# Gate stage of a two-layer encoder: staged weights fetched one set ahead, the low halves of the gate weights on VectorE, the cast of the merged activations one chunk later

## The chip, the cores and the metric

The kernel runs on one NeuronCore of a Trainium2 chip. The metric is the device time of one execution in microseconds (us); the median of three runs is given. Engines: PE (TensorE, matmuls), DVE (VectorE), ACT (ScalarE), POOL (GpSimd) and SP (SyncE, which here only issues transfers). Each engine takes its instructions in the order of the program and waits on semaphores for the others.

## The reference, cut to what matters

Two consecutive layers over 1,056 tokens (1,024 of a prompt, 32 of a running stream), 1,024 channels, float32. The part around the change is the merge behind attention (branch a) and spatial gating (branch b):

```
q, k, v, qi, ki, wi, u, vg, ga, gb = split(x @ w_in)
merged = sigmoid(ga) * (o_a @ w_pa) + sigmoid(gb) * (o_b @ w_pb)
x = LN1(ALPHA * x + merged @ w_out)
x = LN2(ALPHA * x + square(relu(x @ w_ff1)) @ w_ff2)
```

## The kernel before, in words

**Numbers.** Every matrix operand is cut into a high half (the value cast to fp32r) and a low half (value minus high half). A product takes three matmuls: high x high, high x low, low x high (`mac3`, L563 to L565).

**Tiles.** Activations lie channel by token, tokens in three chunks of 384, 384 and 288 columns. `gemm` takes one group of 128 output columns of the weights at a time (a group m), and in it chunk by chunk: all matmuls of a chunk into one PSUM bank of pool `mm` (two banks), then `evac`, which empties the bank, then some steps of a side job (`stage.step`).

**Stages of a layer.** The front (input projections, top-k selection, attention) is laid out by a planner, `Sched`. It takes task costs and priorities from the tables `CFG` (entry 0 for layer 0, entry 1 for layer 1) and writes each engine's order. Behind it stands the gate stage, written by hand in `gate_phase`: a rest of gb (one group), PB (`o_b @ w_pb`, 8 groups of 4 x 128 rows, emptied by DVE at L1792), PA (`o_a @ w_pa`, 8 groups of 4 x 128 rows, emptied by ACT at L1798) and GA (ga, 8 groups of 8 x 128 rows). Then `mixer_tail` runs five groups of `w_out` by `gemm` (emptied by DVE at L1822 and L1823) and hands the rest to the planner: last groups, norm and the MLP.

**GA's emptying.** For each chunk ACT writes the sigmoid of the bank to a work tile (L1807), DVE multiplies by PA's result and adds the gb term (L1808, L1809), and ACT casts the sum to the high half of `merged` (L1810). After the third chunk of a group DVE makes the three low halves (L1815).

**Weights.** `Stream` (`ws`) brings the weights of all these groups. `get` cuts the group after the present one and fetches the one after that: a transfer on SP's queue into one of two raw tiles (L482), then on POOL a copy for the high half (L460) and a subtraction for the low half (L468) into one of four `slab` tiles.

**The staged sums.** `Stage` is the side job: for the MLP's second matrix it loads 24 sets of four 128-row blocks by 256 columns (two transfers, L1736), makes four sums on DVE (L1746, L1747, L1749, L1750), casts the high halves on ACT (L1755), makes the low halves on DVE (L1759) and stores both to `wD` in device memory (four transfers, L1760, L1761). A set takes five steps; PB and PA run one step a chunk, GA and w_out two. Its tiles come from the pool `st` of seven buffers, handed out in turn: two raw, two high and two low per set. The transfer of the next set is issued in step 4 of the present one, behind its stores on SP.

Of the kernel before, what the change touches and what calls it, by code (L numbers as in the profile page):

```python
# [54 lines left out]
class T:  # L55
    pass


CFG = [{'PRI': {'iw': -0.263,
          'ck': -1.41,  # L60
          'ix': 0.646,
          'ie': 7.629,
          'sc': -1.88,
          'sb': 0.12,
          'sa': -3.806,
          'w0': -12.158,
          'w1': -20.884,
          'q0': 0.818,
          'q1': -0.506,
          'qe': -2.132,  # L70
          'qf': -10.943,
          'vw': -2.371,
          'vg': 0.964,
          'kw': -0.64,
          'kv': 17.749,
          'ke': -2.247,
          've': 6.527,
          'kf': -0.064,
          'sg': -6.589,
          'sh': -2.689,  # L80
          'sv': -3.979,
          'uw': 3.518,
          'u': 1.569,
          'gw': 22.568,
          'g': 8.705,
          'tk': 13.75,
          'ta': 1.653,
          'tb': 0.012,
          'td': 0.218,
          'tu': 1.174,  # L90
          'tm': 0.821,
          'tv': 0.272719516,
          'ca': -16.039,
          'cb': -3.477,
          'at': -0.61,
          'un': 0.057,
          'qk': -4.73,
          'lm': -6.346,
          'ex': -1.74,
          're': -5.398,  # L100
          'no': 6.46,
          'tr': 4.284,
          'pc': -13.59,
          'ps': 1.194,
          'pv': 6.416,
          'fi': 1.481,
          'fo': -7.008,
          'fg': 39.227,
          'fh': 9.693,
          'fw': 1.109,  # L110
          'fe': -3.641,
          'if': -3.311,
          'lt': -3.992,
          'lc': -5.237,
          'nb': 4.366,
          'nz': -7.65,
          'lv': 2.538,
          'rd': -15.758},
  'ORDER': [2, 4, 0, 3, 8, 1, 6, 5, 7],
  'IORD': [0, 5, 1, 4, 2, 3, 8, 6, 7],  # L120
  'QORD': [4, 8, 7, 3, 5, 2, 0, 6, 1],
  'KORD': [8, 3, 2, 1, 5, 7, 0, 4, 6],
  'CR': [0, 1, 2],
  'PEN': {'V': 0.82161371, 'S': 0.30937078, 'G': 0.0},
  'XPR': [4.187073758, -18.133365959, -0.385257991],
  'GLATE': 10,
  'BXK': 'mm|lg',
  'P13': 'pt',
  'P12': 'buf',
  'P11': 'buf',  # L130
  'TPK': 'tp|mm',
  'FLK': 'tp|mm',
  'BKK': 'tp|tp',
  'SGK': 'tp|lg',
  'MMK': 'mm|tp|lg',
  'MTK': 'tp|lg',
  'PVK': 'mm|tp|lg'},
 {'PRI': {'iw': 1.116,
          'ck': -1.329,
          'ix': 0.495,  # L140
          'ie': 3.337,
          'sc': -3.797,
          'sb': 0.152,
          'sa': -3.277,
          'w0': -12.127,
          'w1': 2.962,
          'q0': 1.662,
          'q1': -8.268,
          'qe': 1.253,
          'qf': -17.089,  # L150
          'vw': 6.706,
# [24 lines left out]
          'qk': -10.595,
          'lm': 22.428,
          'ex': 4.959,
          're': -5.159,
          'no': 1.164,  # L180
          'tr': -3.253,
          'pc': 1.243,
          'ps': -3.243,
          'pv': 10.918,
          'fi': 4.409,
          'fo': -0.689,
          'fg': 5.578,
          'fh': 4.434,
          'fw': 6.004,
          'fe': -4.622,  # L190
          'if': 0.401,
          'lt': 11.598,
          'lc': 20.451,
          'nb': -16.84,
          'nz': -16.864,
          'lv': -6.918,
          'rd': 5.965},
  'ORDER': [5, 4, 2, 0, 8, 1, 3, 7, 6],
  'IORD': [3, 1, 0, 4, 2, 8, 5, 6, 7],
  'QORD': [6, 5, 7, 0, 3, 1, 8, 2, 4],  # L200
  'KORD': [1, 5, 7, 0, 2, 4, 8, 3, 6],
  'CR': [0, 1, 2],
  'PEN': {'V': 0.810300138, 'S': 0.563224975, 'G': 0.448262313},
  'XPR': [-2.402896891, -8.136167056, -1.136631082],
  'GLATE': -1,
  'BXK': 'tp|lg',
  'P13': 'pt',
# [142 lines left out]
def tile_trunk(ctx: ExitStack, tc: tile.TileContext, I, O):  # L350
# [118 lines left out]

    class Stream:  # L470
        def __init__(self):
            self.items, self.used, self.dmas, self.splits, self.raws, self.out = [], 0, 0, 0, {}, {}
# [13 lines left out]
        def cut(self, i):  # L486
            while self.splits <= i:
                j = self.splits
                self.fetch(j)
                _, kt, ncol, _, place = self.items[j]  # L490
                n, raw = kt * ncol, self.raws.pop(j)
                if place is not None:
                    hi, lo = [xrow(8 * place + 4 * i, 4)[:, :, 2 * CH:2 * CH + 256] for i in range(2)]
                    split(hi, lo, raw.rearrange("p (a c) -> p a c", a=4), "g", "g")
                    self.out[j] = [[x[:, k // 2, k % 2 * 128:(k % 2 + 1) * 128] for k in range(KT)] for x in (hi, lo)]
                    self.splits += 1
                    continue
# [5 lines left out]
                split(hi, lo, raw, "g", "g")  # L503
                self.out[j] = [[x[:, k * ncol:(k + 1) * ncol] for k in range(kt)] for x in (hi, lo)]
                self.splits += 1

        def get(self, ahead=1):
            i = self.used
            self.used += 1
            self.cut(i)  # L510
            for j in range(i + 1, min(i + 1 + ahead, len(self.items))):
                if self.items[j][3]:
# [66 lines left out]
    def rhs_x(k, t0, n):  # L579
        return xh(k, t0, n), xl(k, t0, n)  # L580
# [1142 lines left out]
    class Stage:  # L1723
# [14 lines left out]
            self.fetched += 1  # L1738

        def steps(self):  # L1740
            for n, (c, mp) in enumerate(self.todo):
                if n == 0:
                    self.fetch()
                t = self.raw.pop((c, mp))
                q = [t[0][:, :, 0:128], t[1][:, :, 0:128], t[0][:, :, 128:256], t[1][:, :, 128:256]]
                V.tensor_tensor(q[3], q[2], q[3], op=OP.add)  # L1746
# [6 lines left out]
                h = [half_t("st", F32R)[:, 0:512].rearrange("p (k c) -> p k c", k=2) for _ in range(2)]  # L1753
# [12 lines left out]
        def step(self, n):  # L1766
# [2 lines left out]

    def gate_phase(L):  # L1770
        st = L.st = Stage(L.l)
        obh = hb_t(F32R)
        obl = [row_t(i, F32R) for i in LAYOUT_LO]
        for i in range(4):
# [25 lines left out]
        L.mh = a_t(F32R)  # L1800
        L.mhi = [L.mh[:, m, :] for m in range(KT)]
        L.mlo = []
        held = []

        def ev(m, t0, n, ps):
            w = work([128, CH])[:, :n]
            S.activation(w, ps, AF.Sigmoid)  # L1807
            V.tensor_tensor(w, w, p2[m][:, t0:t0 + n], op=OP.mult)  # L1808
            V.tensor_tensor(w, w, g2[m][:, t0:t0 + n], op=OP.add)  # L1809
            S.copy(L.mhi[m][:, t0:t0 + n], w)  # L1810
            held.append((t0, n, w))
            if len(held) == 3:
                L.mlo.append(row_t(LAYOUT_HI[m], F32R))
                for t0, n, w in held:
                    V.tensor_tensor(L.mlo[m][:, t0:t0 + n], w, L.mhi[m][:, t0:t0 + n].bitcast(F32), op=OP.subtract)  # L1815
                held.clear()
        gemm(KT, KT, rhs_x, ev, st)

    def residual(R):
        def ev(m, t0, n, ps):  # L1820
# [174 lines left out]
    def mixer_tail(L):  # L1995
# [524 lines left out]
```

## Time and profile before

| | us |
|---|---|
| median of three runs | 3130.18 (3125.76 to 3131.55) |
| the profiled execution | 3129.05 |
| its span, first to last instruction | 3127.3 |
| PE busy in it | 2944.9 (94%) |
| DVE busy | 2148.6 (69%) |
| ACT busy | 1370.9 (44%) |
| POOL busy | 829.0 (27%) |

The profile is of one execution. Its time is the span and about 2 us around it. A busy PE is not PE at its peak: matmuls are pipelined, and their durations overlap. So a stage is best judged by how long it takes for its number of matmuls. PEclk is the share of its full clock that PE was granted. A row of a window holds: from and to, its length, busy time (and number of instructions) of PE, PEld (PE's weight loads), DVE, ACT and POOL, PEclk, the busy share of the DMA engines and GB/s.

### The profile page before, as it was taken

The page shows a single profiled execution, that of the slowest core. Times are in us where ns is not written, and L with a number is a line of the kernel's source. Part 1 is how long each engine was busy: PE and PEld are TensorE (multiplying, and loading weights), DVE is VectorE, ACT ScalarE, POOL GpSimd, SP SyncE. Part 2 cuts the span into 40 slices and gives each one's busy share as a digit, 9 for nine tenths or more (in the row PEclk, how much of TensorE's full clock was granted, in tenths as well). Part 3 has the DMA queues.
Part 4 walks back from the last instruction along what each step waited for, and adds up shares of the span by engine and source line. Part 5 has one row for each costly group of instructions (what it writes and reads, how often), then busy time and mean ns, then how long its engine had stood idle before and what let it go on. Part 6 is the DMA issues. An engine that isn't in the chain of part 4 may idle for free.

```text
span 3127.3 us, 54780 instructions
## 1 busy us (share of the span) xinstructions
PE 2944.9 (94%) x20868; PEld 2874.2 (92%) x20868; DVE 2148.6 (69%) x4416; ACT 1370.9 (44%) x2702; POOL 829.0 (27%) x1191
## 2 busy tenths in 40 slices
PE   8999898988999999999999999989889999999998
PEld 7998898987899999999989999879788999999998
DVE  6888874465676648885479887844656766488845
ACT  5687663221343325442347865722213433254422
POOL 5733532322200001111376324433223000011023
PEclk9999999999999999999989999999899999999999
DMA  3101104545353328564111111045453533285642
GB/s 113 46 28 36 46 21 139 185 155 168 100 176 110 102 92 290 183 207 137 32 40 48 45 29 42 12 152 182 145 175 104 165 110 110 94 290 191 200 127 83
DMA packets 336023, 368.77 MB, mean 118 GB/s; under 512 B 32656, under 2 KB 257936, under 8 KB 335760
## 3 DMA queue, kind: packets, MB, share of 16 engines
q1 hardware_dynamic: 335760, 365.27, 36.6%
q8 instruction: 164, 2.69, 0.4%
q14 instruction: 99, 0.81, 0.1%
HBM read 259.05 MB, written 106.15 MB: 117 GB/s over the span
## 4 chain that ended last, share of the span: by engine, by line
PE 60%; DVE 13%; DMA 9%; ACT 3%; issue 3%; SPq 2%; POOL 2%; POOLq 0%; DVEq 0%; ACTq 0%
PE lg L1905 17%; PE tp L1905 8%; DMA st<-in_w_ff_dram 5%; PE mm L563 5%; PE mm L565 5%; PE mm L564 5%; PE mm L1905 4%; PE lg L563 2%; PE lg L565 2%; PE lg L564 2%; DVE st L1759 1%; ACT junk_a L943 1%; PE lg L1063 1%; PE lg L1064 1%; DVE J L908 1%
## 5 line engine op out<-in xcount | busy, mean ns | idle before, releaser
L943 ACT ACTIVATE junk_a<-R,sel 128x640 int8<-128x640 f32 (+6 forms) x258 | 226.3, 877 | 61.3 <-DVE sel L956 54.7
L460 POOL TENSOR_SCALAR sl<-rw 128x1024 fp32r<-128x1024 f32 (+1 forms) x92 | 90.2, 981 | 605.0 <-PE mm L564 227.1
L564 PE MATMUL mm<-R,sl 128*128 128x384 f32 (+1 forms) x722 | 236.9, 328 | 13.9 <-DVE R L1815 11.7
L563 PE MATMUL mm<-A,sl 128*128 128x384 f32 (+1 forms) x512 | 168.3, 329 | 12.6 <-DVE HB L1822 9.8
L651 POOL TENSOR_TENSOR HB<-w,HB 128x528 fp32r<-128x528 f32 x2 | 2.6, 1321 | 637.8 <-ACT HB L464 637.8
L1746 DVE TENSOR_TENSOR st<-st,st 128x256 f32<-128x256 f32 x48 | 27.1, 564 | 206.9 <-DMA st<-in_w_ff_dram 206.9
L908 DVE TENSOR_SCALAR_CACHE_REDUCE J<-R,sel 128x896 uint8<-128x896 f32 (+6 forms) x190 | 167.2, 890 | 2.4
L565 PE MATMUL mm<-A,sl 128*128 128x384 f32 (+1 forms) x512 | 166.1, 324 | 0.4 <-POOL sl L468 0.4
L468 POOL TENSOR_TENSOR sl<-rw,sl 128x1024 fp32r<-128x1024 f32 (+1 forms) x77 | 153.6, 1994 | 17.4 <-PE tp L1103 4.5
L1755 ACT CAST st<-st 128x512 fp32r<-128x512 f32 x96 | 56.8, 618 | 224.9 <-DVE st L1749 194.6
L563 PE MATMUL mm<-XB,sl 128*128 128x384 f32 (+1 forms) x456 | 153.5, 337 | 0.0
L564 PEld LDWEIGHTS mm<-R,sl 128*128 128x128 f32 x722 | 139.2, 193 | 15.1 <-DVE R L1815 12.3
L564 PE MATMUL mm<-XB,sl 128*128 128x384 f32 (+1 forms) x456 | 152.2, 334 | 0.0
L565 PE MATMUL mm<-XB,sl 128*128 128x384 f32 (+1 forms) x444 | 148.5, 335 | 0.0
L2344 DVE TENSOR_TENSOR A<-lg,A 128x528 f32<-128x528 f32 x168 | 118.4, 705 | 40.3 <-PE lg L1905 38.1
L1905 PE MATMUL lg<-R,sl 128*128 128x264 f32 x1024 | 144.1, 287 | 1.8 <-DVE A L2342 1.6
L1905 PEld LDWEIGHTS lg<-R,sl 128*128 128x128 f32 x1024 | 134.0, 191 | 2.6 <-DVE A L2342 2.0
L1091 POOL TENSOR_SCALAR sl<-sl,sm 128x640 f32<-128x640 f32 (+8 forms) x90 | 71.0, 796 | 169.1 <-DVE sm L1087 139.0
L563 PEld LDWEIGHTS mm<-A,sl 128*128 128x128 f32 x512 | 97.4, 190 | 16.3 <-DVE HB L1822 8.3
L563 PE MATMUL mm<-HB,sl 128*128 128x384 f32 (+1 forms) x262 | 88.6, 338 | 19.3 <-DVE R L1792 14.6
L2152 ACT COPY st<-lg 128x528 f32<-128x528 f32 x72 | 43.2, 600 | 142.1 <-PE lg L1905 112.5
L1905 PE MATMUL lg<-R,A 128*128 128x264 f32 x816 | 104.9, 284 | 0.0
(818 smaller groups left out, 10162.6 us busy)
## 6 DMA issues: line engine op xcount, KB each, us to landing
rw<-in_w_ff_dram SPq DMA_DIRECT2D x104, 512.0 KB, 4.7
wD<-st SPq DMA_DIRECT2D x192, 256.0 KB, 2.5
rw<-in_w_in_dram SPq DMA_DIRECT2D x60, 512.0 KB, 4.4
R<-wD SPq DMA_DIRECT2D x50, 512.0 KB, 4.5
hD<-st SPq DMA_DIRECT2D x94, 264.0 KB, 2.1
st<-in_w_ff_dram SPq DMA_DIRECT2D x96, 256.0 KB, 4.0
sl<-wD SPq DMA_DIRECT2D x46, 512.0 KB, 3.9
st<-hD SPq DMA_DIRECT2D x72, 264.0 KB, 5.6
```

Source lines behind the costliest of these rows:

```text
L460: G.tensor_scalar(o, i, 1.0, 1.0, op0=OP.mult, op1=OP.mult)
L468: {"g": G, "v": V}[e_lo].tensor_tensor(lo, src, hi.bitcast(F32), op=OP.subtract)
L563: PE.matmul(ps, ah, bh, start=first, stop=False)
L564: PE.matmul(ps, ah, bl, start=False, stop=False)
L565: PE.matmul(ps, al, bh, start=False, stop=last)
L908: V.tensor_scalar(junk[j % 2].bitcast(U8)[:p, :n], L.sc(b), thr, None, op0=op, op1=OP.add, accum_out=g.cnt[:p, j:j + 1])
L943: S.activation(junk_a[:p, :n], L.sc(b), AF.Sign, bias=g.cf[:p, j:j + 1], scale=-1.0, accum_out=g.cnt[:p, j:j + 1])
L1091: ENG[eng].tensor_scalar(self.lt[e], self.lt[e], self.ms[:, 2, e:e + 1], 1.0, op0=OP.mult, op1=OP.mult)
L1755: S.copy(h[j], t[j])
L1905: PE.matmul(bank[name, s], a[:, k, :], b, start=fresh and k == 0 and i == 0, stop=k == kt - 1 and i == 2, skip_group_check=not fresh)
L2152: S.copy(both(bx[key]), bank["B"])
L2344: V.tensor_tensor(r, b, r, op=OP.add)
```

## The change

Five edits:

- `Stage`: the first set's load is issued as before, and each set now begins with its two high tiles and the load of the set after it. The low halves overwrite the raw tiles, so a set takes four `st` buffers. The stores stand one step later than the low halves.
- `Stream`: while `late` is set (the gate stage and the five groups of w_out), POOL only copies; the subtraction goes to DVE by `follow`, which `gemm` calls after each chunk and `get` at its start. This moves 30 subtractions per layer (16 of 512 columns, 14 of 1,024).
- GA: ACT's cast of a chunk (`his_out`) stands behind the next chunk's sigmoid, and DVE's three low halves of a group (`lows_out`) behind the first add of the next group.
- `mixer_tail` clears `late` after the staged sums are done.
- The priority tables `CFG[0]` and `CFG[1]` have other numbers. In layer 0's front this changes the mixing of gb projections with attention; in layer 1 hardly any row of PE moves.

```diff
-  'BXK': 'mm|lg',
+  'BXK': 'tp|mm',
...
+                if self.late:
+                    copy("g", hi, raw)
+                    self.low.append((lo, raw, hi))
+                else:
+                    split(hi, lo, raw, "g", "g")
...
+        def follow(self):
+            for lo, raw, hi in self.low:
+                V.tensor_tensor(lo, raw, hi.bitcast(F32), op=OP.subtract)
+            self.low.clear()
...
                 if stage:
                     stage.step(kt // 4)
+                ws.follow()
...
         def steps(self):
-            for n, (c, mp) in enumerate(self.todo):
-                if n == 0:
-                    self.fetch()
+            self.fetch()
+            for c, mp in self.todo:
+                h = [half_t("st", F32R)[:, 0:512].rearrange("p (k c) -> p k c", k=2) for _ in range(2)]
+                self.fetch()
...
                 for j in range(2):
-                    lo = half_t("st", F32R)[:, 0:512].rearrange("p (k c) -> p k c", k=2)
-                    V.tensor_tensor(lo, t[j], h[j].bitcast(F32), op=OP.subtract)
+                    V.tensor_tensor(t[j], t[j], h[j].bitcast(F32), op=OP.subtract)
+                yield
+                for j in range(2):
                     nc.sync.dma_start(w[:, 0, 2 * j:2 * j + 2], h[j].bitcast(F32))
-                    nc.sync.dma_start(w[:, 1, 2 * j:2 * j + 2], lo.bitcast(F32))
-                self.fetch()
-                yield
+                    nc.sync.dma_start(w[:, 1, 2 * j:2 * j + 2], t[j])
...
+        def his_out():
+            for m, t0, n, w in his:
+                S.copy(L.mhi[m][:, t0:t0 + n], w)
+            his.clear()
...
         def ev(m, t0, n, ps):
             w = work([128, CH])[:, :n]
             S.activation(w, ps, AF.Sigmoid)
             V.tensor_tensor(w, w, p2[m][:, t0:t0 + n], op=OP.mult)
             V.tensor_tensor(w, w, g2[m][:, t0:t0 + n], op=OP.add)
-            S.copy(L.mhi[m][:, t0:t0 + n], w)
-            held.append((t0, n, w))
...
+            his_out()
+            if t0 == 0:
+                lows_out()
+            his.append((m, t0, n, w))
+            held.append((m, t0, n, w))
         gemm(KT, KT, rhs_x, ev, st)
+        his_out()
+        lows_out()
```

SP's queue in layer 0's PB, before: stores of one staged set (`wD`), then the load of the next (`st`), then weights (`rw`).

```order
L1736 DMA st_6313<-in_w_ff_dram 128x2x256
L1736 DMA st_6314<-in_w_ff_dram 128x2x256
L482 DMA rw_6350<-in_w_pb_dram 128x4x128
L1760 DMA wD_6382<-st_6383 128x512
L1761 DMA wD_6382<-st_6401 128x512
L1760 DMA wD_6382<-st_6384 128x512
L1761 DMA wD_6382<-st_6405 128x512
L1736 DMA st_6409<-in_w_ff_dram 128x2x256
L1736 DMA st_6410<-in_w_ff_dram 128x2x256
```

The same place now (L1747 is the load, L1772 and L1773 the stores).

```order
L1747 DMA st_6250<-in_w_ff_dram 128x2x256
L1747 DMA st_6251<-in_w_ff_dram 128x2x256
L482 DMA rw_6292<-in_w_pb_dram 128x4x128
L1772 DMA wD_6287<-st_6248 128x512
L1773 DMA wD_6287<-st_6244 128x512
L1772 DMA wD_6287<-st_6249 128x512
L1773 DMA wD_6287<-st_6245 128x512
L1747 DMA st_6345<-in_w_ff_dram 128x2x256
L1747 DMA st_6346<-in_w_ff_dram 128x2x256
```

The pattern on the queue is the same, but the stores of a set (here st_6244 to st_6249) now stand behind the load of the set after it (st_6250, st_6251), and are followed by the load of the one after that.

DVE in the same stage, before (L1792 empties a bank; the rest are staged sums).

```order
L1759 TENSOR_TENSOR st_6305<-st_6245,st_6282 128x512
L1759 TENSOR_TENSOR st_6309<-st_6246,st_6283 128x512
L1792 TENSOR_TENSOR R_894_5910<-mm_6317,R_894_5910 128x384
L1792 TENSOR_TENSOR R_894_5910<-mm_6331,R_894_5910 128x288
L1746 TENSOR_TENSOR st_6314<-st_6313,st_6314 128x2x128
L1747 TENSOR_TENSOR st_6313<-st_6313 128x2x128
L1792 TENSOR_TENSOR R_923_6123<-mm_6352,R_923_6123 128x384
```

And now (L1803 empties a bank, L513 is the low half of a group of weights, L1769 the low halves of a staged set).

```order
L1769 TENSOR_TENSOR st_6244<-st_6244,st_6248 128x512
L1769 TENSOR_TENSOR st_6245<-st_6245,st_6249 128x512
L513 TENSOR_TENSOR sl_6290<-rw_6228,sl_6290 128x512
L1803 TENSOR_TENSOR R_895_5902<-mm_6311,R_895_5902 128x384
L1803 TENSOR_TENSOR R_895_5902<-mm_6329,R_895_5902 128x288
L1758 TENSOR_TENSOR st_6251<-st_6250,st_6251 128x2x128
L1759 TENSOR_TENSOR st_6250<-st_6250 128x2x128
L1803 TENSOR_TENSOR R_923_6123<-mm_6355,R_923_6123 128x384
```

One subtraction per group has come into DVE's order, behind the group's first emptying.

ACT in layer 0's GA, before (L1807 sigmoid, L1810 cast of the merged chunk, L1755 cast of a staged set).

```order
L1807 ACTIVATE w_7268<-mm_7243 128x384
L1810 CAST A_7194<-w_7268 128x384
L1807 ACTIVATE w_7302<-mm_7277 128x288
L1810 CAST A_7194<-w_7302 128x288
L1755 CAST st_7312<-st_7239 128x512
L1755 CAST st_7313<-st_7240 128x512
L1807 ACTIVATE w_7359<-mm_7334 128x384
```

And now (L1831 sigmoid, L1818 the cast, L1766 the staged set's).

```order
L1831 ACTIVATE w_7247<-mm_7222 128x384
L1818 CAST A_7180<-w_7211 128x384
L1831 ACTIVATE w_7287<-mm_7262 128x288
L1818 CAST A_7180<-w_7247 128x384
L1766 CAST st_7252<-st_7140 128x512
L1766 CAST st_7253<-st_7141 128x512
L1831 ACTIVATE w_7327<-mm_7302 128x384
```

The cast behind a sigmoid is now that of the chunk before (w_7247 behind the sigmoid of w_7287).

## Rows read from the trace of the kernel before

**Rows 1.** Windows: PB, PA, GA, w_out of layer 0, then of layer 1.

```profile
503.80:561.50 57.70, 50.93 (x288) 49.03 (x289) 30.00 (x52) 5.83 (x10) 18.76 (x19) 0.94 0.51 158
561.50:610.40 48.90, 46.76 (x288) 45.92 (x289) 20.49 (x27) 15.17 (x32) 17.44 (x14) 1.00 0.65 200
610.40:729.10 118.70, 101.11 (x579) 98.77 (x578) 72.02 (x120) 29.87 (x64) 28.91 (x16) 0.93 0.50 159
729.10:799.20 70.10, 60.62 (x361) 58.82 (x361) 41.31 (x71) 9.38 (x16) 18.07 (x10) 0.98 0.59 174
2057.80:2119.40 61.60, 51.19 (x290) 48.78 (x289) 31.32 (x51) 7.89 (x13) 18.12 (x19) 0.95 0.48 150
2119.40:2166.20 46.80, 46.38 (x290) 46.07 (x290) 18.06 (x27) 14.83 (x31) 16.88 (x14) 1.00 0.68 207
2166.20:2287.80 121.60, 102.91 (x577) 100.89 (x577) 73.22 (x119) 29.98 (x64) 28.24 (x16) 0.92 0.47 149
2287.80:2361.00 73.20, 61.25 (x363) 59.78 (x362) 41.55 (x71) 9.38 (x16) 18.05 (x10) 0.93 0.58 172
```

**Rows 2.** Waits of PE, 503 to 800 and 2057 to 2362: total, times, longest.

```profile
PE mm L563 <- ACT w L1807: 17.6, 8, 5.8
PE mm L563 <- DVE R L1792: 6.0, 6, 2.7
PE mm L564 <- DVE R L1815: 4.4, 1, 4.4
...
PE mm L563 <- ACT w L1807: 18.7, 7, 6.2
PE mm L563 <- DVE R L1792: 9.3, 5, 3.5
PE mm L564 <- DVE R L1815: 7.2, 1, 7.2
```

**Rows 3.** Waits of DVE, 503 to 800.

```profile
DVE st L1746 <- DMA st<-in_w_ff_dram: 99.5, 24, 6.7
```

**Rows 4.** Timeline of one stall in GA: start, duration, what, idle before.

```profile
652.06 0.43 DVE L1746 TENSOR_TENSOR st<-st,st 128x256 f32<-128x256 f32 x1 [4.56 <-DMA st<-in_w_ff_dram]
...
653.83 1.41 POOL L460 TENSOR_SCALAR sl<-rw 128x1024 fp32r<-128x1024 f32 x1 [10.35 <-DMA rw<-in_w_in_dram]
654.37 1.27 DVE L1809 TENSOR_TENSOR w<-w,R 128x384 f32<-128x384 f32 x1
...
655.67 0.51 ACT L1810 CAST A<-w 128x384 fp32r<-128x384 f32 x1 [7.24 <-DVE w L1809]
...
657.58 0.44 PE L563 MATMUL mm<-XA,sl 128*128 128x384 f32 x1 [3.93 <-ACT w L1807]
...
659.01 0.52 PE L564 MATMUL mm<-XB,sl 128*128 128x384 f32 x1
```

**Rows 5.** DMA view, 503 to 800: count, KB each, median us from issue to landing.

```profile
wD<-st SPq DMA_DIRECT2D x96, 256.0 KB, 2.4
st<-in_w_ff_dram SPq DMA_DIRECT2D x48, 256.0 KB, 4.0
...
rw<-in_w_pb_dram SPq DMA_DIRECT2D x6, 256.0 KB, 4.3
```

**Rows 6.** Timeline of SP in PB.

```profile
528.65 0.99 SPq L1736 DMA_DIRECT2D st<-in_w_ff_dram  x2
```

**Rows 7.** Groups by form, 500 to 800, DVE and POOL: busy, mean ns of one.

```profile
L1750 DVE TENSOR_TENSOR st<-st,st 128x256 f32<-128x256 f32 x24 | 20.6, 859 | 0.8
...
L468 POOL TENSOR_TENSOR sl<-rw,sl 128x1024 fp32r<-128x1024 f32 x14 | 34.6, 2468 | 1.2
```

**Rows 8.** Two lines of DVE by source: ns shortest/median/longest, 128x1024 and 128x512.

```profile
L651 DVE TENSOR_TENSOR sl<-rw,sl x6: 1214/1221/1744, 53.8 to 467.8; 128x1024 fp32r<-128x1024 f32 x6
...
L1759 DVE TENSOR_TENSOR st<-st,st x48: 673/684/1812, 515.1 to 792.7; 128x512 fp32r<-128x512 f32 x48
```

**Rows 9.** Window of layer 0's attention; columns as in the first group.

```profile
270.00:494.00 224.00, 205.38 (x1380) 196.20 (x1379) 171.87 (x426) 148.50 (x329) 86.21 (x107) 0.97 0.11 32
```

More of the change, by code (lines that the diff above doesn't have):

```diff
@@ L56 @@
     pass
[L59 to L63, printed above, removed]
-          'sb': 0.12,
[L65 to L87, printed above, removed]
+CFG = [{'PRI': {'iw': -1.62,
+          'ck': -2.534,
+          'ix': -0.922,
+          'ie': 11.512,
+          'sc': -2.998,
+          'sb': 0.12,
+          'sa': -5.094,
+          'w0': -8.956,
+          'w1': -18.937,
+          'q0': 0.794,
+          'q1': -1.805,
+          'qe': -2.579,
+          'qf': -9.035,
+          'vw': -3.962,
+          'vg': 1.121,
+          'kw': -1.771,
+          'kv': 17.147,
+          'ke': -3.045,
+          've': 7.406,
+          'kf': -0.498,
+          'sg': -0.208,
+          'sh': -0.379,
+          'sv': -8.711,
+          'uw': 3.742,
+          'u': 2.691,
+          'gw': 27.018,
+          'g': 11.368,
+          'tk': 12.542,
+          'ta': 1.717,
           'tb': 0.012,
@@ L90 @@
           'tu': 1.174,
[L91 to L103, printed above, removed]
[L104 to L118 removed]
+          'tm': 0.996,
+          'tv': 0.27798616,
+          'ca': -15.577,
+          'cb': -1.405,
+          'at': -0.533,
+          'un': 0.049,
+          'qk': 2.076,
+          'lm': -7.861,
+          'ex': -1.321,
+          're': -2.508,
+          'no': 8.104,
+          'tr': 5.696,
+          'pc': -13.893,
+          'ps': 1.194,
+          'pv': 5.819,
+          'fi': 1.591,
+          'fo': -6.643,
+          'fg': 38.129,
+          'fh': 8.711,
+          'fw': 2.038,
+          'fe': -4.065,
+          'if': -3.311,
+          'lt': -9.478,
+          'lc': -2.014,
+          'nb': 4.504,
+          'nz': -17.743,
+          'lv': 1.599,
+          'rd': -18.738},
   'ORDER': [2, 4, 0, 3, 8, 1, 6, 5, 7],
[L120 to L122 removed]
+  'IORD': [2, 1, 5, 4, 0, 3, 8, 6, 7],
+  'QORD': [0, 8, 7, 5, 3, 4, 6, 1, 2],
+  'KORD': [8, 3, 0, 5, 1, 7, 2, 4, 6],
   'CR': [0, 1, 2],
[L124 to L125 removed]
+  'PEN': {'V': 0.82161371, 'S': 0.297213529, 'G': 0.0},
+  'XPR': [1.712330499, -18.413104909, -4.295057706],
   'GLATE': 10,
[L127 removed]
+  'BXK': 'tp|mm',
   'P13': 'pt',
@@ L130 @@
   'P11': 'buf',
-  'TPK': 'tp|mm',
+  'TPK': 'mm|tp|lg',
   'FLK': 'tp|mm',
@@ L189 @@
[L189 to L193, printed above, removed]
+          'no': 0.197,
+          'tr': -3.066,
+          'pc': 0.392,
+          'ps': -3.26,
+          'pv': 10.392,
+          'fi': 4.409,
+          'fo': 4.686,
+          'fg': 5.712,
+          'fh': 4.257,
+          'fw': 7.127,
+          'fe': -6.737,
+          'if': -0.021,
+          'lt': 11.893,
+          'lc': 14.853,
           'nb': -16.84,
-          'nz': -16.864,
@@ L471, in __init__ @@
         def __init__(self):
-            self.items, self.used, self.dmas, self.splits, self.raws, self.out = [], 0, 0, 0, {}, {}
+            self.items, self.used, self.dmas, self.splits, self.raws, self.out, self.late, self.low = [], 0, 0, 0, {}, {}, False, []
         def add(self, pieces, kt, ncol, bar=False, place=None):
@@ L509, in get @@
             self.used += 1
+            self.follow()
             self.cut(i)
@@ L1771, in gate_phase @@
         st = L.st = Stage(L.l)
+        ws.late = True
         obh = hb_t(F32R)
@@ L1802, in gate_phase, with lows_out @@
         L.mlo = []
-        held = []
+        held, his = [], []
+        def his_out():
+            for m, t0, n, w in his:
+                S.copy(L.mhi[m][:, t0:t0 + n], w)
+            his.clear()
+        def lows_out():
+            if held:
+                m = held[0][0]
+                L.mlo.append(row_t(LAYOUT_HI[m], F32R))
+                for _, t0, n, w in held:
+                    V.tensor_tensor(L.mlo[m][:, t0:t0 + n], w, L.mhi[m][:, t0:t0 + n].bitcast(F32), op=OP.subtract)
+                held.clear()
         def ev(m, t0, n, ps):
@@ L2007, in mixer_tail @@
         L.st.step(1000)
+        ws.follow()
+        ws.late = False
         use(2)
```

88 lines of the change are left out of this document (37 added, 51 removed).

## The prediction

> **What bounds the kernel now.** I split the trace into stages by the first matmul of each, and read the windows of the gate stage and of w_out first [rows 1]. PA is the yardstick: 288 matmul rows in 46.8 us in layer 1, PE clock 1.00, nothing to wait for. That is 1.95 us a chunk. PB has as many matmuls of the same sizes, GA twice as many, the five w_out groups 5/4 as many. Without stalls they would take 46.8, 93.6 and 58.5 us. They take:
>
> - layer 0: PB 57.7, PA 48.9, GA 118.7, w_out 70.1, which is 10.9 + 2.1 + 25.1 + 11.6 = 49.7 us over;
> - layer 1: 61.6, 46.8, 121.6, 73.2, which is 14.8 + 0 + 28.0 + 14.7 = 57.5 us over.
>
> So 107 us of 3129 are lost here, and no engine but PE is near its limit: in GA of layer 0 DVE is busy for 72.0 of 118.7 us.
>
> Next come the waits of PE [rows 2]. In GA it waits for ACT's sigmoid (17.6 and 18.7 us), in PB for DVE's emptying (6.0 and 9.3), at the start of w_out for the last low halves (4.4 and 7.2). Those are 63 of the 107 us. The reader should ask why ACT and DVE are late when neither is full. DVE's own waits answer [rows 3]: it waits for the load of each staged set, 24 times, 99.5 us in layer 0. The timeline shows how that reaches PE [rows 4]: DVE gets its data at 652.06 after 4.56 us, the add L1809 stands behind the sums, ACT's cast L1810 waits 7.24 us for that add, the next sigmoid stands behind the cast, and PE, both banks full, stops for 3.93 us. The load is late because it is issued in step 4 and used two steps later: two chunks of PB, 3.9 us, against 4.0 us from issue to landing [rows 5].
>
> A stall costs twice. The granted clock is 0.92 to 0.95 in PB and GA, and 1.00 in PA [rows 1]. In the timeline PE stops until 657.58, and the matmul at 659.01 already takes 0.52 us [rows 4], the 1.2 GHz level. At most (1 - PEclk) times the window is lost so: 3.5 + 8.3 + 1.4 us in layer 0, 3.1 + 9.7 + 5.1 in layer 1, 31 us together. With 63 us of waits that explains 94 of the 107; the rest are waits too short to stand among these rows.
>
> **The change part by part.**
>
> *The load one set ahead.* It is issued behind the stores of the set before last, so its price is set by SP. Once a set's low halves are done, SP issues four stores and two loads. Two loads take 0.99 us [rows 6]; I take 2.0 for four stores. The load overwrites a tile that the last store reads, so SP waits for that store, 2.4 us, then issues the loads (1.0), which land 4.0 us later [rows 5]. That is 9.4 us after the low halves. The sums that use it come seven steps after them (step 4 of one set to step 1 of the next but one): 7 x 1.95 = 13.6 us in PB, and as much in GA, where two steps share a chunk of 3.9 us. So 4.2 us are to spare. DVE's 99.5 us of waiting should go, but for the first set of each layer. I take a rest of 1 us per layer on PE.
>
> *Cast a chunk later, low halves a group later.* ACT's next sigmoid no longer stands behind a DVE add of its own chunk. PE waits for a sigmoid only if ACT or DVE falls back by more than a chunk. At the end of GA the three last low halves come after two staged steps, later in DVE's order than before; but PE needs the first of them only when it reaches the last eighth of w_out's first chunk, 3.4 us on. I take 1 us of wait there instead of 4.4 and 7.2.
>
> *Weights' low halves on DVE.* DVE takes 1.22 us for 1,024 columns and 0.68 for 512 [rows 8]: 14 x 1.22 + 16 x 0.68 = 28 us more per layer. On POOL a large one took 2.47 [rows 7]. Does DVE have room? Per group, from its busy time [rows 1]: GA 72.0 / 8 = 9.0, now 10.2 of 11.7 us; w_out 41.3 / 5 = 8.3, now 9.5 of 11.7; PB 30.0 / 8 = 3.8, now 4.4 of 5.85. That is the upper bound, because POOL's subtractions also held DVE up: L1750 averages 859 ns [rows 7], while L1746, of the same form, took 0.43 us undisturbed [rows 4]; that alone is 24 x 0.43 = 10 us. So the 28 us lie beside PE. If PE's cover were gone, they would cost 28 us a layer.
>
> *What is late next.* The new subtraction waits in DVE's order for POOL's copy, and that for the weights' load on SP. In PB a group's load can stand right behind SP's wait for the stores: 2.0 + 2.4 + 1.0 + 0.5 (its own issue) + 4.3 us to land [rows 5, 6], and at most 1.4 for the copy [rows 4], 11.6 us after the staged low halves. Its subtraction stands six chunks behind them, 11.7 us. There is no margin, and DVE's emptying is queued behind; PE has two banks, about two chunks of grace. I take 4 us in PB. In GA a group lasts 11.7 us, so its weights have that much more room. I take 3 us for GA, where DVE is at 87%, 2 for w_out, and 1 for the clock after what stays. Sum of what stays per layer: 1 + 1 + 4 + 3 + 2 + 1 = 12 us.
>
> *A rule against the move.* POOL's copy, too, holds DVE up: in the timeline the add L1809 takes 1.27 us beside the copy of 1.41 us [rows 4], where even 512 columns take 0.68 by the median [rows 8]. The Trainium skill (SBUF — State Buffer, Who interferes with whom) says that a DVE instruction with two SBUF inputs contends with a GpSimd instruction that reads SBUF, and that one blocks for the whole of the other. By that rule the 30 subtractions moved join the DVE work that the 30 copies can block. If every copy blocked DVE for its 1.4 us, GA's group would come to 11.6 of 11.7 us, just under PE; as a whole on the path, 30 x 1.4 us would cost 42 us per layer, and the time would be about 3131. The trace agrees that copies block, but before, subtractions of 2.47 us blocked as well, and those go; so the sum goes without it.
>
> *The tables.* In layer 0's attention window PE is busy for 205.4 of 224 us at clock 0.97 [rows 9]: 18.6 us idle and 6.7 of clock, 25 us in all, is the most that a better mixture can win. A worse one could lose about as much. The rows mix the same pieces differently, without a wait that I can see added or removed, so I take 0 and keep 10 us either way for the range. Layer 1 hardly changes order.
>
> **Sum.** 107 - 2 x 12 = 83 us. The profiled execution took 3129.05; 3129 - 83 = 3046. The median of the runs shown is 1.1 us above it, so 3047.
>
> **The rivals.**
>
> 1. *The wait moves instead of going.* DVE stops waiting for staged loads and waits for weights or stores through SP. For it: SP waits on the stores by construction, and PB has no margin. Against: 4.2 us to spare for staged loads, and the DMA engines are at 0.65 to 0.68 in PA [rows 1] while PE runs without waits. Half of the gain: 3130 - 42 = 3088.
> 2. *DVE becomes the bound in GA and w_out*, because POOL's copies and the added subtractions block each other. For it: 10.2 us of work and 1.4 of blocking in a group of 11.7, before any wait in order. Against: nothing else on POOL is left to block. At one us over PE's 11.7 per group it costs 8 us per layer in GA and 5 in w_out: 3047 + 26 = 3073.
> 3. *Layer 0's front loses* by the other mixture, all it can, 25 us: 3072. It may win as well: 3022.
> 4. *Slower.* The staged loads still land after their step, and now each late set also holds up the next group's weights, since their subtraction stands in the same DVE order. Place: DVE in PB and GA. Price: the 107 us stay, and the 28 us of subtractions per layer come on the path: 3130 + 56 = 3186. It decides if a load lands over 13.6 us after the low halves, 4.2 us later than I work out. In [rows 5] the median is 4.0 in all, so it would have to double.
> 5. *No effect*: the late load was a symptom. Against it stand [rows 3, 4].
>
> **How the numbers follow.** Forecast (3022 to 3066) 0.75; rival 1 0.12; rival 2 0.05; rival 3 0.03; rival 5 0.02; rival 4 0.03. The range must leave out no more than 2 in 10: from 3022 (all of the 107 us gone, 3023, or the front winning its 25) to 3084, which takes in rivals 2 and 3 and part of rival 1. A measurement of this kernel tells about 0.2%, 6 us, from no change. Faster by more: 0.95; within: 0.02; slower: 0.03.
>
> **What the profile of the changed kernel would show.** Right: DVE's wait for st loads falls from about 100 us per layer to under 15; PB near 50, GA near 97, w_out near 61 us; PEclk 0.98 or more in GA; POOL's subtractions gone from the gate stage, and DVE busier in GA in share. Wrong: DVE waiting for POOL's copy or for the load in its place; SP's wait for stores over 4 us each; GA over 105 us with DVE over 95% busy; layer 0's PB starting much before or after 503.8.

## The result and the profile after

The changed kernel takes 3021.61 us (median of four runs, 3018.34 to 3026.95) against 3127.97 for the kernel before on the same chip: a ratio of 0.966, 95% interval 0.964 to 0.968. It is faster, as forecast, by 106 us instead of 83; the time lies 0.4 us under the range's lower end. The forecast started from a kernel before at 3130.18, not 3127.97; that times the ratio gives 3024, inside it. The profiled execution took 3018.34 us, 110.7 less than the 3129.05 of before.

First the same windows as in [rows 1]: PB, PA, GA and w_out of layer 0, then of layer 1.

```profile
503.90:552.80 48.90, 47.87 (x288) 47.43 (x289) 30.42 (x60) 5.71 (x10) 6.57 (x10) 0.97 0.61 194
552.80:598.80 46.00, 46.00 (x291) 46.00 (x290) 21.28 (x39) 14.66 (x31) 5.13 (x8) 1.00 0.74 228
598.80:691.60 92.80, 92.80 (x579) 92.80 (x578) 70.32 (x130) 30.13 (x66) 8.79 (x8) 1.00 0.64 202
691.60:749.40 57.80, 57.80 (x362) 57.56 (x361) 39.35 (x70) 8.24 (x14) 5.33 (x5) 1.00 0.65 197
2006.80:2052.90 46.10, 46.10 (x290) 46.10 (x289) 29.68 (x59) 7.45 (x13) 5.66 (x8) 1.00 0.65 202
2052.90:2098.90 46.00, 46.00 (x291) 46.00 (x290) 22.47 (x39) 14.65 (x31) 6.88 (x9) 1.00 0.79 231
2098.90:2191.70 92.80, 92.80 (x578) 92.80 (x578) 70.63 (x130) 30.03 (x66) 8.07 (x8) 1.00 0.65 201
2191.70:2249.50 57.80, 57.80 (x362) 57.56 (x362) 39.54 (x70) 8.24 (x14) 5.31 (x5) 1.00 0.65 196
```

Layer 0 goes from 295.4 to 245.5 us, layer 1 from 303.2 to 242.7: 49.9 + 60.5 = 110.4 us, all but 0.3 us of the difference of the two profiled executions. Read the second and third numbers of the GA rows together: PE is busy for 92.80 of 92.80 us, at clock 1.00. Nothing stands still there any more. DVE's busy time in GA fell from 72.0 to 70.3 us, although 8 x 1.22 us of subtractions were added.

The waits of PE and of DVE for staged loads in layer 0 (503 to 750) answer to [rows 2, 3]; total, times, longest. The rows of PE are all that there are.

```profile
DVE sl L513 <- POOL sl L460: 8.9, 1, 8.9
PE mm L573 <- POOL sl L460: 3.9, 1, 3.9
DVE st L1758 <- DMA st<-in_w_ff_dram: 1.9, 1, 1.9
PE mm L573 <- DVE R L1803: 1.0, 1, 1.0
```

DVE waits once for a staged load, 1.9 us in place of 24 times and 99.5. PE's waits for the sigmoid and for the last low halves are gone. What is left is the start of PB: its first weights are late, for DVE as for PE. That wait of 3.9 us stands ahead of the first window, and it was there before as well (3.6 and 0.7 us). The 1.0 us lies inside PB and comes from the first staged load: DVE starts that set's sums late, the emptying L1803 stands behind them, and PE waits for it. The timeline of DVE and PE, and the window of PB's first 4 us:

```profile
510.31 0.42 DVE L1758 TENSOR_TENSOR st<-st,st 128x256 f32<-128x256 f32 x1 [1.89 <-DMA st<-in_w_ff_dram]
...
511.72 0.55 DVE L1803 TENSOR_TENSOR R<-mm,R 128x384 f32<-128x384 f32 x1
...
512.41 0.41 PE L573 MATMUL mm<-HB,sl 128*128 128x384 f32 x1 [0.97 <-DVE R L1803]
```

```profile
503.90:508.00 4.10, 4.03 (x15) 3.81 (x16) 0.83 (x2) 0.00 (x0) 1.30 (x3) 0.62 0.52 150
```

After the stop of 3.9 us PE's granted clock is 0.62 over these 4.1 us, which is 4.1 x 0.38 = 1.6 us lost. The two together are 2.6 of the 2.9 us by which PB of layer 0 is longer than PA.

Next the timeline of SP in PB (start, duration, what), and under it DVE's staged instructions of the same stretch.

```profile
522.98 0.50 SPq L1772 DMA_DIRECT2D wD<-st  x1
525.33 0.34 SPq L1773 DMA_DIRECT2D wD<-st  x1
525.76 0.93 SPq L1772 DMA_DIRECT2D wD<-st  x1
526.79 0.38 SPq L1773 DMA_DIRECT2D wD<-st  x1
527.23 0.98 SPq L1747 DMA_DIRECT2D st<-in_w_ff_dram  x2
```

```profile
524.62 1.28 DVE L1769 TENSOR_TENSOR st<-st,st 128x512 f32<-128x512 f32 x2
...
528.90 0.41 DVE L1758 TENSOR_TENSOR st<-st,st 128x256 f32<-128x256 f32 x1
...
538.33 0.41 DVE L1758 TENSOR_TENSOR st<-st,st 128x256 f32<-128x256 f32 x1
```

The low halves of a set end at 525.90. Its last store ends its issue at 527.17, and the loads follow at 527.23, so SP does not wait for that store to land. In the program the only store of the set for which a load waits is the first, and that was issued at 522.98. Over layer 0 the loads' waits for stores come to two, 2.0 us in all, where I had priced 2.4 us for each of the 24 sets. The two loads are out by 528.21, and with the 4.0 us of median landing they are there by about 532.2 (an estimate, worked out from these rows). The sums at 528.90 use the load before; this one is used at 538.33, some 6 us later.

### The profile page after: what moved, and what is told of

Read it like the earlier page. It is cut to its first block, busy times and chain, and to the rows that moved or that the text cites. A ratio compares the mean times of both kernels' runs of the same rounds, so it can differ in the third digit from the quotient of the medians.

```text
span 3016.6 us, 54852 instructions
## 1 busy us (share of the span) xinstructions
PE 2911.2 (97%) x20868; PEld 2852.7 (95%) x20868; DVE 2141.4 (71%) x4473; ACT 1367.8 (45%) x2692; POOL 729.7 (24%) x1144
## 4 chain that ended last, share of the span: by engine, by line
PE 81%; DVE 7%; DMA 3%; POOL 3%; ACT 3%; issue 2%; SPq 0%; POOLq 0%; DVEq 0%; ACTq 0%
PE lg L1929 18%; PE mm L573 10%; PE mm L575 10%; PE mm L574 10%; PE tp L1929 9%; PE mm L1929 5%; PE lg L573 2%; PE lg L575 2%; PE lg L574 2%; PE lg L1074 1%; PE lg L1075 1%; ACT junk_a L954 1%; PE tp L1114 1%; PE tp L573 1%; DVE J L919 1%
## 5 line engine op out<-in xcount | busy, mean ns | idle before, releaser
L954 ACT ACTIVATE junk_a<-R,sel 128x768 int8<-128x768 f32 (+6 forms) x257 | 226.3, 881 | 58.2 <-DVE sel L967 52.7
L573 PE MATMUL mm<-XB,sl 128*128 128x384 f32 (+1 forms) x456 | 149.8, 328 | 0.0
L575 PE MATMUL mm<-XB,sl 128*128 128x384 f32 (+1 forms) x456 | 149.1, 327 | 0.0
L574 PE MATMUL mm<-XB,sl 128*128 128x384 f32 (+1 forms) x456 | 148.5, 326 | 0.0
L1766 ACT CAST st<-st 128x512 fp32r<-128x512 f32 x96 | 55.1, 620 | 166.9 <-DVE st L1761 133.8
L846 ACT ACTIVATE sm<-sm,eps 128x1 f32<-128x1 f32 (+1 forms) x72 | 20.7, 293 | 191.1 <-DVE sm L842 184.4
L1929 PEld LDWEIGHTS lg<-R,A 128*128 128x128 f32 x816 | 101.6, 188 | 0.0
L575 PEld LDWEIGHTS mm<-A,sl 128*128 128x128 f32 x512 | 96.3, 188 | 0.0
L573 PEld LDWEIGHTS mm<-A,sl 128*128 128x128 f32 x512 | 96.2, 188 | 0.0
```

Source lines behind the costliest of these rows:

```text
L573: PE.matmul(ps, ah, bh, start=first, stop=False)
L574: PE.matmul(ps, ah, bl, start=False, stop=False)
L575: PE.matmul(ps, al, bh, start=False, stop=last)
L954: S.activation(junk_a[:p, :n], L.sc(b), AF.Sign, bias=g.cf[:p, j:j + 1], scale=-1.0, accum_out=g.cnt[:p, j:j + 1])
L1929: PE.matmul(bank[name, s], a[:, k, :], b, start=fresh and k == 0 and i == 0, stop=k == kt - 1 and i == 2, skip_group_check=not fresh)
```

## The experiments

All twelve have the edit shown and nothing else. Ratios are to the kernel before, run on the same chip: it took 3127.97 us beside the changed kernel, 3126.84 beside the four with "no", 3125.67 beside stage_only, lead2, lead3 and dve_x3, and 3123.13 beside the other four. Kernels from different groups are therefore best compared by their ratios. Stage lengths are those of layer 0, from the windows of one execution of each kernel, in us; the kernel before and the changed one stand first.

| kernel | time | ratio (95%) | PB | PA | GA | w_out |
|---|---|---|---|---|---|---|
| before | 3127.97 | 1 | 57.7 | 48.9 | 118.7 | 70.1 |
| changed | 3021.61 | 0.966 (0.964 to 0.968) | 48.9 | 46.0 | 92.8 | 57.8 |
| no_tables | 3022.87 | 0.967 (0.964 to 0.969) | 49.2 | 46.0 | 92.8 | 57.8 |
| no_stage | 3114.77 | 0.997 (0.995 to 0.998) | 58.5 | 49.8 | 108.0 | 75.1 |
| no_late | 3023.51 | 0.967 (0.964 to 0.970) | 49.4 | 45.9 | 92.8 | 59.4 |
| no_cast | 3018.15 | 0.965 (0.963 to 0.967) | 49.1 | 45.9 | 92.8 | 57.6 |
| stage_only | 3025.57 | 0.967 (0.965 to 0.969) | 49.5 | 45.9 | 93.7 | 60.3 |
| late_only | 3117.70 | 0.998 (0.997 to 0.999) | 55.8 | 49.9 | 118.8 | 68.4 |
| lead2 | 3020.22 | 0.965 (0.963 to 0.967) | 47.8 | 45.9 | 92.8 | 57.8 |
| lead3 | 3021.81 | 0.966 (0.964 to 0.968) | 48.6 | 45.9 | 92.8 | 57.8 |
| same_queue | 3116.22 | 0.997 (0.995 to 0.998) | 56.8 | 50.6 | 112.9 | 72.6 |
| dve_x2 | 3027.29 | 0.969 (0.967 to 0.970) | 51.6 | 45.9 | 92.8 | 59.2 |
| dve_x3 | 3064.70 | 0.980 (0.978 to 0.981) | 58.5 | 46.0 | 102.2 | 62.1 |
| pb_early | 3014.73 | 0.965 (0.963 to 0.966) | 49.1 | 45.9 | 92.8 | 57.8 |

### One part of the change undone

**no_tables**: the tables `CFG` of before in the changed kernel.

```diff
-  'BXK': 'tp|mm',
+  'BXK': 'mm|lg',
...
```

> The changed kernel with the priority tables of before. Theory (the tables are worth 0 in layer 0's front; the whole gain lies in the gate stage and w_out): 3021 us, 3012 to 3030, and layer 0's PB starts at 503.8 again. Rival (the other mixture in the front helps the gate stage too, by what it leaves on the queues): slower than 3030.

3022.87 us, and the four stages are the same. PB starts at 505.9 instead of 503.9, later than expected. The tables are worth nothing that can be told here.

**no_stage**: the old `steps` in the changed kernel.

```diff
-            self.fetch()
-            for c, mp in self.todo:
-                h = [half_t("st", F32R)[:, 0:512].rearrange("p (k c) -> p k c", k=2) for _ in range(2)]
-                self.fetch()
+            for n, (c, mp) in enumerate(self.todo):
+                if n == 0:
+                    self.fetch()
...
+                    lo = half_t("st", F32R)[:, 0:512].rearrange("p (k c) -> p k c", k=2)
...
+                    nc.sync.dma_start(w[:, 1, 2 * j:2 * j + 2], lo.bitcast(F32))
+                self.fetch()
                 yield
```

> The changed kernel with the staged sums as before: load in step 4, two steps ahead of its use, separate low tiles. Theory (the late load is the cause of most of the 107 us): DVE waits for st loads by about 4 us a set again, PB, GA and w_out stretch, 3095 us (3070 to 3115). It is not all of 107, since ACT's cast no longer stands ahead of the next sigmoid. Rival (the order of cast and sigmoid and the lows on DVE were the cause, DVE's wait is harmless once PE does not hang on it): under 3045.

3114.77 us: just inside the range, and much nearer to the kernel before than I thought. This edit alone takes back 93 of the 106 us. The other two edits are left with GA 10.7 us shorter and w_out 5.0 longer than before.

**no_late**: the weights' subtraction stays on POOL.

```diff
-        ws.late = True
```

> The changed kernel with the weights' subtraction back on POOL. Theory (with the loads early, POOL's blocking of DVE costs DVE time but not PE time): DVE's busy time in GA stays near 70 us or rises though 9.8 us of subtractions leave it, and the time is 3026 (3018 to 3040). Rival (POOL's 2.47 us subtractions late in a group, or their blocking, reach PE): over 3040.

3023.51 us, as the theory said. The window of GA, and in it DVE's addition (L1832 here, L1833 in the changed kernel) for a third chunk beside POOL's subtraction:

```profile
599.00:691.80 92.80, 92.80 (x578) 92.80 (x577) 76.52 (x123) 30.13 (x66) 28.40 (x16) 1.00 0.65 207
```

```profile
612.00 2.49 POOL L468 TENSOR_TENSOR sl<-rw,sl 128x1024 fp32r<-128x1024 f32 x1
```

```profile
608.73 0.56 DVE L1832 TENSOR_TENSOR w<-w,R 128x384 f32<-128x384 f32 x1
612.26 2.55 DVE L1832 TENSOR_TENSOR w<-w,R 128x288 f32<-128x288 f32 x1
```

The smaller of two like instructions takes 2.55 us, as long as POOL's 2.49 beside it, where the larger takes 0.56. It is so in nearly every group. That addition by form from 503 to 750 (busy, mean ns of one), here and in the changed kernel:

```profile
L1832 DVE TENSOR_TENSOR w<-w,R 128x288 f32<-128x288 f32 x8 | 18.3, 2284 | 0.3
...
L1833 DVE TENSOR_TENSOR w<-w,R 128x288 f32<-128x288 f32 x8 | 3.7, 458 | 0.3
```

DVE is busy for 76.5 us in GA with 9.8 us less to do, so blocking costs it some 16 us there (76.5 - 70.3 + 9.8), most of it in this addition (15.7 us for seven in GA, 3.2 in the changed kernel). PE loses nothing by it, 92.80 of 92.80; only w_out is 1.6 us longer.

**no_cast**: GA's emptying as before.

```diff
-            his_out()
-            if t0 == 0:
-                lows_out()
-            his.append((m, t0, n, w))
-            held.append((m, t0, n, w))
+            S.copy(L.mhi[m][:, t0:t0 + n], w)
+            held.append((t0, n, w))
+            if len(held) == 3:
...
```

> The changed kernel with ACT's cast right behind its sigmoid again and the low halves behind the third chunk. Theory (ACT waited long only because DVE did): 3027 (3019 to 3037), the rest being the wait for the last low halves at the start of w_out. Rival (ACT's order is a cause of its own, worth the 17.6 and 18.7 us that PE waited for the sigmoid): 3050 to 3065.

3018.15 us, 0.9 under the theory's range, with the same stages. The order of cast and sigmoid is worth nothing once DVE is on time, and the wait at the start of w_out stays away too.

### One part alone in the kernel before

**stage_only**: the new `steps` in the kernel before, the diff of no_stage the other way round.

> The kernel before with the staged sums' edit alone: the load a set ahead, four st buffers a set, stores a step later. Theory (the late load is the cause): 3045 us (3028 to 3062), DVE's wait for st loads under 15 us per layer. Rival (the three edits of the gate stage need each other, since ACT's cast and POOL's subtractions hold PE up by themselves): 3065 or more.

3025.57 us, better than the theory's range: 100 of the 106 us. What the other edits add shows in w_out, 60.3 against 57.8 us, and is too little for the comparison of times. PE's waits for the sigmoid and for the last low halves in layer 0 (17.6 and 4.4 us before):

```profile
PE mm L564 <- DVE R L1814: 2.4, 1, 2.4
...
PE mm L563 <- ACT w L1806: 0.6, 1, 0.6
```

The first is about the 2.5 us of w_out. It is 1.5 us in no_late and is gone in no_cast, so what is left of it goes with POOL's subtractions: stage_only and no_late have them, no_cast has not.

**late_only**: `Stream`'s and `gemm`'s edits, with `late` set and cleared, in the kernel before.

```diff
+        ws.late = True
...
+                ws.follow()
```

> The kernel before with the weights' subtraction on DVE as the only edit. Theory (with late staged loads the subtraction waits in DVE's order behind sums that wait, and PE waits for the low halves as it does in the run without the staged sums' edit, 15.6 us in layer 0): slower than before, 3138 us (3127 to 3160). Rival (freeing DVE of POOL's 2.47 us subtractions helps by itself): 3095 to 3120.

3117.70 us, ratio 0.997 to 0.999: not slower, so my theory fell. The rival's band ends at 3120 and holds the time, but only because the kernel before took 3123.13 on this chip: 5 us are won, where the rival asked for 8 or more from 3128. PB and w_out win about 2 us each; GA wins nothing. The subtraction does stand behind sums that wait, as these two of PE's waits in layer 0 show:

```profile
PE mm L575 <- DVE sl L513: 16.3, 8, 4.5
...
PE mm L573 <- ACT w L1819: 5.3, 3, 3.4
```

PE waits for these low halves 16.3 us in total. But this takes the place of other waits on the same late DVE: that for the sigmoid falls from 17.6 to 5.3 us. A wait in a row is not an addition to the time when another would have stood there.

### What makes the load late

**lead2** and **lead3**: `fetch` of the next set at the start of step 4, or of step 3, instead of step 1.

```diff
                 h = [half_t("st", F32R)[:, 0:512].rearrange("p (k c) -> p k c", k=2) for _ in range(2)]
-                self.fetch()
...
                     S.copy(h[j], t[j])
                 yield
+                self.fetch()
```

(In lead3 the added line stands one `yield` earlier.)

> The changed kernel with the load of the next set issued at the start of a set's step 4, two steps ahead of its use, all else as changed. Theory (it is the time between issue and use that counts: 3.9 us in PB against 1.0 + 4.0 to land): DVE waits for st loads again, by over 1 us a set, and the time is 3060 (3035 to 3095). Rival (it was the shortage of st tiles and the stores ahead of the load on SP that made it late; with four tiles a set two steps are enough): under 3030.

> The changed kernel with the load issued at the start of a set's step 3, three steps ahead of its use. Theory (5.85 us in PB against 1.0 + 4.0, and no wait for the stores, which are by then long done): still in time, 3022 (3016 to 3032). Rival (the load needs the spare of the whole set): over 3035.

3020.22 and 3021.81 us. For lead3 that was the theory; for lead2 the rival was right, and the time between two steps of the program is not what counts. SP and DVE in lead2's PB:

```profile
527.89 1.31 SPq L1747 DMA_DIRECT2D st<-in_w_ff_dram  x2
...
540.82 1.07 SPq L1747 DMA_DIRECT2D st<-in_w_ff_dram  x2
```

```profile
534.17 1.28 DVE L1769 TENSOR_TENSOR st<-st,st 128x512 f32<-128x512 f32 x2
537.85 0.41 DVE L1757 TENSOR_TENSOR st<-st,st 128x256 f32<-128x256 f32 x1
543.61 1.28 DVE L1769 TENSOR_TENSOR st<-st,st 128x512 f32<-128x512 f32 x2
547.18 0.41 DVE L1757 TENSOR_TENSOR st<-st,st 128x256 f32<-128x256 f32 x1
```

SP runs ahead of the program's steps. It issues the load at 527.89 and 540.82, 6.3 and 2.8 us ahead of the same set's low halves on DVE (534.17, 543.61), because nothing that stands ahead of it on its queue waits for them.

**same_queue**: the changed kernel with the stores in the low halves' step and the next load right behind them, as before, but with four `st` buffers a set. It tells the tiles from the queue.

```diff
-                self.fetch()
                 t = self.raw.pop((c, mp))
...
                     V.tensor_tensor(t[j], t[j], h[j].bitcast(F32), op=OP.subtract)
-                yield
                 for j in range(2):
...
+                self.fetch()
+                yield
                 yield
```

> The changed kernel with SP's order of before in the staged sums (stores in the low halves' step, the next set's load right behind them), but the low halves still in place, so four st buffers a set. With the load two steps ahead but ahead of the set's stores the time was 3020. Theory (what counts is what stands ahead of the load on SP: four stores that wait for this set's low halves): 2.0 + 1.0 + 4.0 us after the low halves against two steps of 1.95, so late in every set, DVE's wait for st loads 60 us or more per layer, 3110 us (3080 to 3125). Rival (six tiles a set out of seven were what made the load late): 3022, under 3040.

3116.22 us: the theory, and no different from no_stage. SP and DVE in PB, and DVE's wait in layer 0:

```profile
526.15 1.36 SPq L1770 DMA_DIRECT2D wD<-st  x1
527.60 0.38 SPq L1771 DMA_DIRECT2D wD<-st  x1
528.03 0.99 SPq L1747 DMA_DIRECT2D st<-in_w_ff_dram  x2
```

```profile
525.01 1.28 DVE L1768 TENSOR_TENSOR st<-st,st 128x512 f32<-128x512 f32 x2
...
533.13 0.42 DVE L1757 TENSOR_TENSOR st<-st,st 128x256 f32<-128x256 f32 x1 [3.33 <-DMA st<-in_w_ff_dram]
```

```profile
DVE st L1757 <- DMA st<-in_w_ff_dram: 82.4, 22, 6.6
```

Low halves until 526.29, loads from 528.03, sums at 533.13 after a wait of 3.33 us: 6.8 us from low halves to sums, where 7.0 were worked out. That chain stood in every set before: DVE waited 24 times for 24 sets. Neither the number of tiles nor the step makes the load late, but the four stores that stand ahead of it and wait for this set's low halves.

### How much room DVE has

**dve_x2** and **dve_x3**: each subtraction of the weights' low halves two or three times, with the same result.

```diff
-                V.tensor_tensor(lo, raw, hi.bitcast(F32), op=OP.subtract)
+                for _ in range(3):
+                    V.tensor_tensor(lo, raw, hi.bitcast(F32), op=OP.subtract)
```

> The changed kernel with each subtraction of the weights' low halves done twice on DVE, 28 us more per layer: a GA group takes 10.0 of 11.6 us, PB 4.5 of 5.75. Once costs nothing, three times 43 us. Theory (a limit: hidden while it fits, then paid): 3028 us (3020 to 3037). Rival (each microsecond of DVE costs its share, by queueing): 3043.

> The changed kernel with each subtraction of the weights' low halves done three times on DVE: 56 us more of DVE per layer. In GA a group then takes DVE 8.8 + 2.4 = 11.2 of 11.6 us, in w_out 10.3, in PB 5.1 of 5.8. Theory (DVE's room hides the moved work while it fits): 3035 (3022 to 3055). Rival (DVE is already at its limit through waits in order): the 56 us come on the path in large part, over 3080.

Twice costs 8 us by the ratios (6 by the times), with intervals that just overlap. Three times costs 43, more than I allowed, and the time stays well under the rival's 3080. PB and GA of dve_x2, then PB and GA of dve_x3, and two waits of PE in layer 0 of dve_x3:

```profile
504.80:556.40 51.60, 49.98 (x289) 48.69 (x290) 37.15 (x69) 5.71 (x10) 6.40 (x9) 0.94 0.57 184
...
602.30:695.10 92.80, 92.80 (x578) 92.80 (x577) 80.45 (x135) 30.34 (x66) 8.94 (x8) 1.00 0.62 199
```

```profile
507.20:565.70 58.50, 51.46 (x289) 49.53 (x289) 43.31 (x79) 5.71 (x10) 7.94 (x9) 0.92 0.51 162
...
611.70:713.90 102.20, 97.12 (x579) 95.36 (x578) 87.77 (x142) 30.90 (x66) 9.93 (x8) 0.97 0.56 177
```

```profile
PE mm L576 <- DVE sl L514: 9.2, 6, 2.6
PE mm L574 <- DVE R L1804: 5.6, 6, 2.0
```

With 80.45 / 8 = 10.1 us of DVE per group GA is still bound by PE alone. With 87.77 / 8 = 11.0 it loses 9.4 us, although PE takes 11.6 for a group. In PB 37.15 / 8 = 4.6 us of DVE per group cost 2.7 us and 43.31 / 8 = 5.4 cost 9.6, both under the 5.75 that PE needs. GA behaves like a limit, PB does not. So the room ends before DVE's busy time reaches PE's: the emptying and the low halves stand behind the rest in DVE's order, each with a time by which PE needs it.

### The wait that is left

**pb_early**: PB's first weights are fetched ahead of the loads of `gD`.

```diff
+        ws.fetch(ws.used + 1)
         for m in range(NGB, NGB + NFG):
             nc.sync.dma_start(g2[m], L.gD[m])
```

> The changed kernel with the first weights of PB fetched ahead of the loads of gD at the start of the gate stage. In the changed kernel they are issued at 496.40 behind three gD loads, land at 503.14, and PE waits 3.9 us at the start of PB. Theory: the wait goes, layer 0's PB starts near 500, 3017.5 us (3013 to 3021). Rival (the raw tile is not free earlier, or the emptying of PB's first bank then waits for gD): no change, 3021.6.

3014.73 us; the interval, 0.963 to 0.966, overlaps that of the changed kernel, so the times do not tell the two apart. PE's waits from 440 to 512:

```profile
PE mm L573 <- DVE R L1804: 1.4, 1, 1.4
PE mm L573 <- ACT R L1796: 0.9, 1, 0.9
```

The 3.9 us are gone, and 0.9 and 1.4 of other waits at the start of PB have taken part of their place. PB and its followers take as long as in the changed kernel (245.6 against 245.5 us), and PB starts at 503.2, 0.7 us earlier than there; this execution was behind by 440 (1006 PE rows from 270 to 440, against 1027). Whether 4 us are won stays open.

## Why the prediction was right, and where it was off

- **What bounds the kernel: right.** The 107 us said to be lost in the gate stage and w_out were 110.4, and all of the gain lies there. Not all that its waits left unexplained was short, though: PE's waits for the emptying of w_out (L1822) came to 5.0 us in layer 0, in a row that it left out.
- **Why the load is late: right in the cause, half right in the reason.** The wait for the staged load is the cause: stage_only brings 100 of 106 us, no_stage loses 93. But "issued in step 4 and used two steps later" is not why; lead2 does the same and is fast. It is the place behind four stores on SP, as same_queue shows.
- **The load one set ahead: right in direction, priced too high.** 9.4 us from low halves to landing became about 6.3 (525.90 to 532.2): the 2.4 us of waiting for the last store's landing did not occur, and of the stores 1.3 us instead of 2.0 lie behind the low halves (525.90 to 527.23), because SP issues the first two before both are done. 4.2 us to spare were some 6. The 1 us of rest holds in layer 0, where DVE's 1.9 us reach PE as 1.0; in layer 1 PE waits for nothing.
- **Cast a chunk later, low halves later: right in size, wrong in what does it.** The waits of 4.4 and 7.2 us at w_out and of 17.6 and 18.7 for the sigmoid are gone, but they stay gone in no_cast. The sigmoid's were echoes of the late load (0.6 us in stage_only). Of the 4.4 at w_out 2.4 stay there; they go with the subtractions that leave POOL.
- **The weights' low halves on DVE: hidden, as said.** GA came to 8.8 us of DVE per group, less than the upper bound of 10.2, because POOL's long subtractions no longer block. The relief of DVE is real (16 us in GA) and of little use to PE (1.6 us in w_out).
- **What is late next: the terms that were mis-sized.** "Sum of what stays per layer: 1 + 1 + 4 + 3 + 2 + 1 = 12 us" was too much. Against the same yardstick the four stages come to 245.5 - 245.7 = -0.2 us in layer 0 and 242.7 - 245.7 = -3.0 in layer 1. The 4 us for PB's weights, the 3 for GA, the 2 for w_out and the 1 for the last low halves were nothing: inside the stages PE waits once in layer 0, for the emptying behind the first staged load, and never in layer 1. The 2.9 us that PB of layer 0 does take over PA (48.9 - 46.0) are that 1.0 us and the clock after the stop ahead of PB, which are the terms "a rest of 1 us" and "1 for the clock". 24 us were forecast and 3 gained instead: that is the 27 us between 83 and 110. Two errors made it. PB's weights were priced with SP's wait for the last store, which does not occur, and GA's 3 was taken from a DVE at 87%, which is at 76% (70.3 of 92.8). With the smaller terms that is some 21 us. And the yardstick, PA of layer 1 at 46.8, was itself 0.8 us longer than PA is now (46.0): the four stages without a wait take 242.7 us, 3.0 less than it gives, 6 us over both layers.
- **The rule against the move.** The Trainium skill (SBUF — State Buffer, Who interferes with whom) says that a DVE instruction with two SBUF inputs contends with a GpSimd instruction that reads SBUF, and that the shared ports are locked for one of the two. The row of 2.55 us beside 2.49 agrees, for the subtraction. As a cost of the move it did not come true: the 30 copies stay, DVE takes 8.8 us per group of GA and not 11.6, and PE waits for nothing there. The copies do hold DVE up, but only for what is left of them when DVE comes: a multiplication of 128x288 that starts at 611.02 beside a copy from 610.49 to 611.68 takes 0.96 us, and one that starts at 635.26, behind its group's copy, takes 0.44.
- **The tables: 0, right.** PB starts within 0.1 us of where it did, and no_tables is no slower.
- **The rivals.** 1 (the wait moves): no. 2 (DVE becomes the bound): no, but nearer than "one us over PE's 11.7 per group": dve_x3 loses 9.4 us in GA at 11.0. 3 (the front loses): no, as no_tables shows. 4 (slower): its condition is far off, and late_only speaks against its price, since there the loads are late and the subtractions stand on DVE, and the time is not longer. 5 (the late load a symptom): no, as stage_only shows.

## What to carry to other kernels

Judge how early a transfer is by what stands ahead of it on its queue and what that waits for, not by the step of the program in which it is written; a load behind stores that wait for this round's last result is late in every round. When one wait has echoes on three engines, mend the wait first: here one edit of five gave 100 of 106 us, and the edits against the echoes gave nothing that the times can tell once it was gone. What stays after such an edit is worth pricing from rows in which the disturbance is absent, else its traces are counted twice.

## What was not expected of the hardware

- SP, which here only issues transfers, ran 3 to 6 us ahead of the engines in the rows shown: in lead2 a load written behind ACT's casts in step 4 was issued at 527.89, while DVE did that set's low halves, the next work in the program, at 534.17.
- DVE became less busy in GA (72.0 to 70.3 us) with 9.8 us more work, since its instructions no longer stand beside POOL's two-input subtraction (2.47 us by the mean before, 2.49 in no_late's row).
- PE's time for a stage without waits hardly varies: GA took 92.8 us in both layers of the changed kernel and in layer 0 of seven others in the table, under DVE loads from 70.3 to 80.5 us.
